# A hybrid encoder layer on one core: both S5 runs one behind the other in the projection phase, beside the delta rule of block 0

## The chip, the core and the metric

The kernel runs on one core of one Trainium2 chip. The core has five engines with a queue each: TensorE (PE, its weight loads PEld), VectorE (DVE), ScalarE (ACT), GpSimd (POOL) and SyncE (SP), whose queue issues the DMAs here. Instructions of one queue start in order; between queues there are semaphores. The metric is the device time of one execution in microseconds, lower is better.

## What is computed

One layer of a streaming encoder for 2048 prompt tokens and 32 sample tokens, in float32, width 1024. All head groups read the same normalised input through one projection:

```python
hn = rmsnorm(h, norm_mix)
qkv_pre, z, ba, u5, cc = split(hn @ w_in)
ya = gdn_mixer(qkv_pre, z, ba, ...)    # A: gated delta rule, 4 heads x 128, state carried along the tokens
yb = s5_mixer(u5, ...)                 # B: 16 x 64 complex states, scan along the tokens, GELU, GLU
yc = conformer_conv(cc, ...)           # C: GLU, causal depthwise convolution of width 31, LayerNorm, swish
h = h + concat([ya, yb, yc]) @ w_out
hf = rmsnorm(h, norm_ffn)
h = h + (silu(hf @ w1) * (hf @ w3)) @ w2        # 22 x 128 hidden columns
h = h + (p @ pe_w) * sigmoid(h @ pe_gate)
y = rmsnorm(h, norm_final)
```

Outputs are y for both token groups and the last states of the three mixers.

## The kernel before

**Blocks and phases.** The prompt is cut into four blocks of 512 tokens (NB = 4); the 32 sample tokens ride with block 3, whose rows are 544 wide. A first phase (PhaseA) projects block after block with w_in; a second (PhaseF) does output projection, FFN and gated embedding, block after block. Between them stand the heads: the conformer (`conformer_block`), the delta rule (`gdn_group`, two groups of 256 tokens per block, one more for the sample tokens behind block 3) and S5 (`s5_unit`, one run for two blocks, G.UB = 2, so G.NU = 2 runs). The delta rule and S5 carry a state, so their blocks come in order. Everything passes between phases through DRAM: `G.us` to S5, `G.xcd` to the conformer, `G.sild` to the delta rule, `G.mixT[b]` from the heads to the output projection of block b.

**Matmuls.** Each projection (`dense`, L122) is three passes of float32r matmuls with 512 columns: high weight half by high input half, low by high, high by low. The high half of a weight is made on ScalarE (L94). The low half is subtracted (L98) by GpSimd, for w3 by VectorE, when a weight is first used, that is in block 0; it is then kept in DRAM and loaded in later blocks. A projection's result lies in one of three PSUM banks (`psD`) until VectorE or ScalarE has read it.

**What sets the order.** Heads are Python generators (chains). `dense` counts the columns that it issues; each time these reach `G.stage` (7168, and 9216 in block 0 of PhaseF), every chain goes one step on, and `yield k` makes a chain wait k steps. `G.flush` runs chains on without columns between until its condition holds. Instructions recorded so are then set in each engine's queue by a scheduler that goes by priorities and by its own estimate of when operands are there; so a head's instructions can stand some way from where they were recorded.

**Chains before.** In PhaseA one chain sets up S5's constants, opens the S5 memory (`R("s5_0")`, a pool named w5 here), and in it runs conformer and delta rule of block 0. From block 2 on a second chain runs S5 for blocks 0 and 1 in that memory. `G.flush()` finishes both. In PhaseF one chain goes on: conformer 1, delta rule 1, conformer 2, S5 for blocks 2 and 3 (in a memory of its own), delta rule 2, conformer 3, delta rule 3 with the sample tokens. Block b of PhaseF starts after `ready[0] >= b`.

**Lines that the prediction speaks of.** L826 (L827 after the change) is the conformer's convolution: 62 VectorE instructions per block, each on half of the 256 channels, written `cacc<-xc,cc_w,cacc`; its input `xc` is loaded at L813. They stand in VectorE's queue among the additions that empty PSUM: L1173 (`hb<-hb,ps_d`, output projection), L1196 to L1204 (hidden columns), L1218 (down projection), L1242 and L1243 (gate). L78 makes the low halves `fal` of the FFN's inputs, L1167 the sum of squares, and L134 spreads the resulting scale. L1069 to L1109 (`ps_vn` to `ps_ot`) are the end of the delta rule. S5's matmuls are L468 (`ps_v`), L526 and L527 (`ps_y`) and L556 (`ps_glu`). L668 is the first matmul of a block in PhaseA; its inputs `hh` and `hl` are made by L77 and L78 into the pool `xp`.

Of the kernel before, what the change touches and what calls it, by code (L numbers as in the profile page):

```python
# [423 lines left out]
def s5_unit(G, A, u, wp, pspool):  # L424
# [14 lines left out]
    for jq in range(4):  # L439
# [15 lines left out]
        Gm = ld("G", [P, 2, 2, P], G.s5c["G"][:, js])  # L455
        Toep = ld("Toep", [P, 4, P], G.s5c["Toep"][:, jq * 4:jq * 4 + 4])

        yield 3

        w = [wp.tile([P, 2, NCT], F32, tag=f"w{i}", name=f"w{i}") for i in range(2)]  # L460
        tm = [wp.tile([P, 2, NCT], F32, tag=f"tm{i}", name=f"tm{i}") for i in range(4)]
# [50 lines left out]
                else:  # L512
                    V.tensor_copy(S1[half[h], js, i], X[h][half[i], :, NC])

        yield 4

        ys = wp.tile([P, 4, NCT], F32, tag="ys", name="ys")
        ysv = ys.rearrange("p (j h) c -> p j h c", h=2)
# [17 lines left out]
        jh = jq // 2  # L536
# [7 lines left out]
        nc.scalar.activation(t, t, AF.Tanh, scale=math.sqrt(2.0 / math.pi))  # L544
        nc.scalar.activation(yf, yf, AF.Copy, scale=0.25)
        V.scalar_tensor_tensor(gq[:, jh], t, 1.0, yf, op0=ALU.add, op1=ALU.mult)
        yield 1 if jh == 0 else 5
    spc = 512 // NCT
    for j in range(2):
        yb = wp.tile([P, n], F32, tag="yf", name="yb")  # L550
# [12 lines left out]
        for i in range(G.UB):  # L563
            b = u * G.UB + i
# [7 lines left out]
class PhaseA:  # L572


    def __init__(self, G, A, ctx):
        self.G, self.A = G, A
        nc = G.nc
        V = nc.vector
        E = lambda name, bufs=1, **k: ctx.enter_context(G.tc.tile_pool(name=name, bufs=bufs, side="left", reuse_waits="tile", **k))
        self.wp = E("aw", 2)  # L580
        self.xp = E("ax", 12)
        cp = E("ac")

        def const(nm, shp, src):
            t = cp.tile(shp, F32, tag=nm, name=nm)
            nc.sync.dma_start(t, src)
            return t

        self.gm = const("gmix", [P, KD], A.norm_mix)
        self.cw = G.cw  # L590
        wr = G.wraw.tile([P, KD, 8], F32, tag="wr", name="wr_ba")
        nc.sync.dma_start(wr, A.w_ba)
        self.wba = cp.tile([P, KD, 16], F32R, tag="wba", name="wba")
        nc.scalar.activation(self.wba[:, :, 0:8], wr, AF.Copy)
        nc.gpsimd.tensor_tensor(self.wba[:, :, 8:16], wr, self.wba[:, :, 0:8].bitcast(F32), op=ALU.subtract)
        self.tails = cp.tile([P, 12, 3], F32, tag="tails", name="tails")
        nc.gpsimd.memset(self.tails, 0.0)
        self.taild = const("taild", [P, 12, 3], A.st_gconv)
# [34 lines left out]
    def block(self, b):  # L633
        G, A, wp = self.G, self.A, self.wp
# [71 lines left out]
        for j, ur in enumerate(urs):  # L706
            u = wp.tile([P, L5, n // L5], F32, tag="gacc", name="u5")
            V.tensor_tensor(u, ur.rearrange("p (c s) -> p s c", s=L5), bc.rearrange("p (c s) -> p s c", s=L5), op=ALU.mult)
            co = (b % G.UB) * BLK // L5
            nc.sync.dma_start(G.us[b // G.UB][:, j * P:(j + 1) * P, co:co + n // L5].rearrange("s p c -> p s c"), u)  # L710

        for j in range(2):
            wg = load_weight(G, A.w_in[20 + j], KD, "ccg", j)
# [544 lines left out]
def trunk_kernel(ctx: ExitStack, tc: tile.TileContext, A):  # L1258
    nc = tc.nc
    G = Ctx()  # L1260
# [16 lines left out]
            tc.cur_priority = G.pr[old]  # L1277

    G.chains = []
    G.acc = 0  # L1280

    def advance(c):
# [28 lines left out]
    NB = G.NB  # L1311
    E = lambda name, bufs=1, **k: ctx.enter_context(tc.tile_pool(name=name, bufs=bufs, **k))
# [59 lines left out]
    R = lambda name, bufs=1: tc.tile_pool(name=name, bufs=bufs, side="right", reuse_waits="tile")  # L1372

    def conf(b, wp):
        return conformer_block(G, A, b, wp, G.psM)

    def gdn_part(b, i, S, sp):
        S = yield from gdn_group(G, A, sp, G.psM, G.tp_, b * 4 + 2 * i, P, 2, S, b, 256 * i)
        if b == NB - 1 and i == 1:
            nc.sync.dma_start(A.gdn_p, S)  # L1380
            Sd = G.kp.tile([P, NH, P], F32, tag="S", name="Sd0")
            nc.sync.dma_start(Sd, A.st_gdn)
            Sd = yield from gdn_group(G, A, sp, G.psM, G.td_, 0, TS, 1, Sd, b, BLK)
            nc.sync.dma_start(A.gdn_s, Sd)
        return S
# [3 lines left out]
    def conf_of(b):  # L1389
        with R(f"cc_{b}") as wp:  # L1390
            yield from conf(b, wp)

    def s5_of(u):
        with R(f"s5_{u}") as wp:
            yield from s5_unit(G, A, u, wp, G.psM)

    def gdn_of(b):
        with R(f"gd_{b}", 2) as sp:
            for i in range(2):
                state[0] = yield from gdn_part(b, i, state[0], sp)  # L1400

    def run(*gens):

        for g in gens:
            yield from g

    with ExitStack() as cx:
        pa = PhaseA(G, A, cx)
        pa.block(0)

        box = {}

        def first_s5():
            while "w5" not in box:
                yield 1
            yield from s5_unit(G, A, 0, box["w5"], G.psM)
            box["done"] = True

        def first_heads():
            with R("s5i") as tp:  # L1420
                yield from s5_init(G, A, tp, G.psM)
            with R("s5_0") as w5:
                box["w5"] = w5
                yield from conf_of(0)
                yield from gdn_of(0)
                while "done" not in box:
                    yield 1

        G.start(first_heads())
        for b in range(1, NB):  # L1430
            if b == G.UB:
                G.start(first_s5())
            pa.block(b)
        if NB == G.UB:
            G.start(first_s5())
        G.flush()
    pf = PhaseF(G, A, ctx)
    ready = [0]

    def later_heads():  # L1440
        for b in range(1, NB):
            yield from conf_of(b)
            if b % G.UB == 0:
                yield from s5_of(b // G.UB)
            yield from gdn_of(b)
            ready[0] = b

    G.start(later_heads())
    for b in range(NB):
        G.flush(lambda: ready[0] >= b)  # L1450
        G.stage = STAGE.get(b, STAGE["A"])
        pf.block(b)

# [114 lines left out]
```

## Time and profile before

| | |
|---|---|
| median of 3 runs | 2884.57 us (2880.83 to 2887.48) |
| profiled execution | 2888.11 us, its span 2886.3 us, mean granted clock 0.979 |
| TensorE busy | 2763.9 us (96%) |
| VectorE busy | 1751.6 us (61%) |
| ScalarE, GpSimd busy | 935.2 us (32%), 549.4 us (19%) |
| DMA queue of SyncE | 562.7 MB, 60.4% of 16 engines' span |
| TensorE on the chain that ended last | 64%, of it the projections L122 57% |

PhaseA ends at about 682 us, and the blocks of PhaseF at about 1231, 1779, 2320 and 2886 us. The page gives busy time per engine, then the span in 40 slices (each digit tenths of a slice), then groups of instructions by line, engine and tiles (`out<-in`, x the count). A busy TensorE is not TensorE at its peak, since a matmul's shown time overlaps the next one's; so stretches are best read by how many matmuls they hold and how long they last. A row of a wait gives the engine and the line that waited, what released it, total us, times, and the longest.

### The profile page before, as it was taken

How to read it: one execution, taken by the hardware profiler on the slowest of the kernel's cores; microseconds unless marked ns; L12 is line 12 of the kernel's file. 1: busy time of each engine (PE TensorE's matmuls, PEld its weight loads, DVE VectorE, ACT ScalarE, POOL GpSimd, SP SyncE). 2: the span in 40 equal slices, each digit the busy share in tenths (PEclk: the TensorE clock that was granted, in tenths of full speed). 3: DMA queues.
4: the chain of work that ended last, by engine and by line, in shares of the span. 5: the costliest groups of instructions: out<-in, count | busy, mean ns of one | idle time of the engine just before them, and what ended most of it. 6: DMA issues, size and time to landing. Idle time of an engine off the chain costs nothing.

```text
span 2886.3 us, 41015 instructions
## 1 busy us (share of the span) xinstructions
PE 2763.9 (96%) x15300; PEld 2359.9 (82%) x15300; DVE 1751.6 (61%) x3933; ACT 935.2 (32%) x1409; POOL 549.4 (19%) x460
## 2 busy tenths in 40 slices
PE   7899999999999999899999999999999979999997
PEld 5668778898878887688888887778888869999997
DVE  8969765865675847966563755856464733333343
ACT  4243423313422222343422333342332423222232
POOL 5731312234232323421010101000010110000000
PEclk9999999999999999999999999999999979999998
DMA  6578777657654555487665657566565654555553
GB/s 225 170 252 269 248 227 227 199 181 245 206 185 167 190 168 200 152 288 220 216 183 176 187 174 242 187 207 192 172 193 154 197 193 149 174 175 176 175 187 107
DMA packets 278919, 565.32 MB, mean 196 GB/s; under 512 B 67344, under 2 KB 126880, under 8 KB 278576
## 3 DMA queue, kind: packets, MB, share of 16 engines
q1 hardware_dynamic: 278720, 562.70, 60.4%
q8 instruction: 121, 1.98, 0.3%
q14 instruction: 78, 0.64, 0.1%
HBM read 457.76 MB, written 104.25 MB: 195 GB/s over the span
## 4 chain that ended last, share of the span: by engine, by line
PE 64%; DVE 8%; DMA 3%; issue 3%; SPq 1%; ACT 1%; POOL 0%; DVEq 0%; POOLq 0%; ACTq 0%
PE ps_d L122 57%; DVE cacc L826 3%; PE ps_kk L935 1%; PE ps_q L1013 1%; PE ps_z L1026 1%; DVE ct L982 1%; DVE cx L983 1%; DVE hb L1218 1%; DMA xd<-cx 1%; DMA hb<-mixT 1%; PE ps_vn L1069 0%; PE ps_o L1083 0%; PE ps_o L1084 0%; PE ps_s L1076 0%; PE ps_ks L1056 0%
## 5 line engine op out<-in xcount | busy, mean ns | idle before, releaser
L94 ACT ACTIVATE wh_w<-wr_w 128x1024 fp32r<-128x1024 f32 (+1 forms) x272 | 281.3, 1034 | 762.9 <-PE ps_d L122 551.4
L122 PE MATMUL ps_d<-fah,wh_w 128*128 128x512 f32 (+1 forms) x1760 | 379.4, 354 | 7.4 <-DVE fa L1196 2.9
L122 PE MATMUL ps_d<-fal,wh_w 128*128 128x512 f32 (+1 forms) x1760 | 376.5, 353 | 0.0
L122 PE MATMUL ps_d<-fah,wl_w 128*128 128x512 f32 (+1 forms) x1760 | 376.1, 353 | 0.0
L122 PEld LDWEIGHTS ps_d<-fah,wh_w 128*128 128x128 f32 x1760 | 291.1, 189 | 53.6 <-issue 4.0
L122 PEld LDWEIGHTS ps_d<-fal,wh_w 128*128 128x128 f32 x1760 | 291.4, 189 | 43.2
L122 PEld LDWEIGHTS ps_d<-fah,wl_w 128*128 128x128 f32 x1760 | 291.3, 189 | 43.2 <-issue 0.4
L1218 DVE TENSOR_TENSOR hb<-hb,ps_d 128x512 f32<-128x512 f32 (+1 forms) x240 | 139.7, 583 | 167.1 <-PE ps_d L122 166.7
L122 PE MATMUL ps_d<-acth,wh_w 128*128 128x512 f32 (+1 forms) x880 | 210.3, 355 | 9.1 <-DVE hb L1218 7.7
L122 PE MATMUL ps_d<-acth,wl_w 128*128 128x512 f32 (+1 forms) x880 | 210.1, 354 | 0.0
L122 PE MATMUL ps_d<-actl,wh_w 128*128 128x512 f32 (+1 forms) x880 | 208.6, 354 | 0.0
L826 DVE SCALAR_TENSOR_TENSOR cacc<-xc,cc_w,cacc 128x512 f32<-128x512 f32 (+1 forms) x240 | 189.4, 824 | 0.0
L122 PEld LDWEIGHTS ps_d<-acth,wh_w 128*128 128x128 f32 x880 | 148.6, 189 | 34.7 <-DVE hb L1218 6.1
L122 PEld LDWEIGHTS ps_d<-actl,wh_w 128*128 128x128 f32 x880 | 149.4, 189 | 22.2
L122 PEld LDWEIGHTS ps_d<-acth,wl_w 128*128 128x128 f32 x880 | 149.2, 189 | 22.2
L98 POOL TENSOR_TENSOR wl_w<-wr_w,wh_w 128x1024 fp32r<-128x1024 f32 (+1 forms) x46 | 108.2, 2351 | 253.9 <-ACT wh_w L94 226.3
L1201 DVE SCALAR_TENSOR_TENSOR fth<-ps_d,bc 128x512 f32<-128x512 f32 (+1 forms) x110 | 64.8, 589 | 132.0 <-PE ps_d L122 131.3
L1196 DVE TENSOR_TENSOR fa<-ps_d,bc 128x512 f32<-128x512 f32 (+1 forms) x110 | 64.5, 588 | 118.5 <-PE ps_d L122 109.4
L122 PE MATMUL ps_d<-hh,wh_qkv 128*128 128x512 f32 (+1 forms) x480 | 107.2, 365 | 13.8 <-DVE raw L615 13.0
L1204 DVE TENSOR_TENSOR actl<-fa,acth 128x512 fp32r<-128x512 f32 (+1 forms) x110 | 81.3, 739 | 51.3 <-ACT acth L1203 50.9
L1199 DVE SCALAR_TENSOR_TENSOR fa<-fth,fa 128x512 f32<-128x512 f32 (+1 forms) x110 | 73.1, 667 | 58.8 <-ACT fth L1198 58.6
L122 PE MATMUL ps_d<-hh,wl_qkv 128*128 128x512 f32 (+1 forms) x480 | 105.5, 361 | 2.3 <-POOL wl_qkv L98 2.3
(479 smaller groups left out, 4783.3 us busy)
## 6 DMA issues: line engine op xcount, KB each, us to landing
wr_w<-in_w SPq DMA_DIRECT2D x256, 512.0 KB, 4.3
wl_w<-lo_w SPq DMA_DIRECT2D x192, 512.0 KB, 4.0
lo_w<-wl_w SPq DMA_DIRECT2D x64, 512.0 KB, 2.9
wr_qkv<-in_w_in SPq DMA_DIRECT2D x48, 512.0 KB, 4.7
wl_qkv<-lo_qkv SPq DMA_DIRECT2D x36, 512.0 KB, 4.2
wr_out<-in_w_out SPq DMA_DIRECT2D x32, 512.0 KB, 5.2
wr_gate<-in_pe_gate SPq DMA_DIRECT2D x32, 512.0 KB, 4.3
wl_out<-lo_out SPq DMA_DIRECT2D x24, 512.0 KB, 5.9
```

The costliest lines, as they stand in the source:

```text
L94: nc.scalar.activation(wh, wr, AF.Copy)
L98: e.tensor_tensor(wl, wr, wh.bitcast(F32), op=ALU.subtract)
L122: nc.tensor.matmul(ps[:, :cn], a[:, i, :], x(k)[:, c0:c0 + cn], start=start and p_ == 0 and i == 0, stop=stop and p_ == 2 and i == K - 1)
L826: V.scalar_tensor_tensor(acc[:, j], xc[:, j, t:t + W], cn_.w[:, j, t:t + 1], acc[:, j], op0=ALU.mult, op1=ALU.add)
L935: nc.tensor.matmul(kk4[:, h - h0], kq[:, 2 * h, cw], kq[:, 2 * h:2 * h + 2, cw], start=True, stop=True)
L982: V.tensor_tensor(t, cx[:, 0:nq, j:j + 1].to_broadcast(sh), cu[:, j:j + 1, j + 1:].to_broadcast(sh), op=ALU.mult)
L983: V.tensor_tensor(cx[:, 0:nq, j + 1:], cx[:, 0:nq, j + 1:], t, op=ALU.subtract)
L1196: V.tensor_tensor(a, p1[:, :cn], bc[:, cs], op=ALU.mult)
L1199: V.scalar_tensor_tensor(a, th, 1.0, a, op0=ALU.add, op1=ALU.mult)
L1201: V.scalar_tensor_tensor(th, p3[:, :cn], 0.5, bc[:, cs], op0=ALU.mult, op1=ALU.mult)
L1204: V.tensor_tensor(fb[:, cs], a, fa[:, cs].bitcast(F32), op=ALU.subtract)
L1218: V.tensor_tensor(hb[m][:, c0:c0 + cn], hb[m][:, c0:c0 + cn], p_[:, :cn], op=ALU.add)
```

## The change

Both S5 runs are made by one chain (`s5_chain`) in one memory, w5. It starts before block 2 of PhaseA; a run starts when the blocks that it needs have been projected, for which PhaseA counts them (`G.u5`). The heads chain (`heads_chain`) runs conformer and delta rule of block 0 beside it, holds w5 until both runs are through, and only then goes on with conformer 1, delta rule 1 and so on; S5 no longer stands between conformer 2 and delta rule 2. The second phase starts when block 0's heads and the first run are ready. Three of the waits inside a run are one step shorter. The pool of PhaseA's input halves has 11 buffers for each half where it had 12.

```diff
@@ s5_unit
-        yield 3
+        yield 2
...
-        yield 4
+        yield 3
...
-        yield 1 if jh == 0 else 5
+        yield 1 if jh == 0 else 4
@@ PhaseA
-        self.xp = E("ax", 12)
+        self.xp = E("ax", 11)
...
+        G.u5 = b + 1
@@ trunk_kernel
+    box = {"ready": -1, "runs": 0}
+
+    def s5_chain():
+        while "w5" not in box:
+            yield 1
+        for u in range(G.NU):
+            while G.u5 < (u + 1) * G.UB:
+                yield 1
+            yield from s5_unit(G, A, u, box["w5"], G.psM)
+            box["runs"] = u + 1
+
+    def ready(b):
+        return box["ready"] >= b and box["runs"] * G.UB > b
+
+    def heads_chain():
+        with R("s5i") as tp:
+            yield from s5_init(G, A, tp, G.psM)
+        with R("s5_0") as w5:
+            box["w5"] = w5
+            yield from conf_of(0)
+            yield from gdn_of(0)
+            box["ready"] = 0
+            while box["runs"] < G.NU:
+                yield 1
+        for b in range(1, NB):
+            yield from conf_of(b)
+            yield from gdn_of(b)
+            box["ready"] = b
...
-        G.start(first_heads())
+        G.start(heads_chain())
         for b in range(1, NB):
-            if b == G.UB:
-                G.start(first_s5())
+            if b == min(G.UB, NB - 1):
+                G.start(s5_chain())
             pa.block(b)
...
-        G.flush()
+        G.flush(lambda: ready(0))
...
-            yield from conf_of(b)
-            if b % G.UB == 0:
-                yield from s5_of(b // G.UB)
-            yield from gdn_of(b)
-            ready[0] = b
...
-        G.flush(lambda: ready[0] >= b)
+        G.flush(lambda: ready(b))
```

Line numbers behind `PhaseA.block`'s new line are one higher than before, up to the chains.

The first place is VectorE's queue in block 0 of PhaseF, from the last output projection to the scale for the hidden columns: `hb` is the addition, `fal` the low halves, `ssum` the sum of squares, `rms_v` to `rso` the scale. Before:

```order
L1173 TENSOR_TENSOR hb<-hb,ps_d 128x512
L98 TENSOR_TENSOR wl_w_7324<-wr_w_7321,wh_w_7323 128x1024
L1167 TENSOR_TENSOR ssum_6921<-ssum_6921,sq_7222 128x512
L78 SCALAR_TENSOR_TENSOR fal<-hb,g_6861,fah 128x512 x5
L1173 TENSOR_TENSOR hb<-hb,ps_d 128x512
L78 SCALAR_TENSOR_TENSOR fal<-hb,g_6861,fah 128x512 x2
L1167 TENSOR_TENSOR ssum_6921<-ssum_6921,sq_7263 128x512
L78 SCALAR_TENSOR_TENSOR fal<-hb,g_6861,fah 128x512
L864 SCALAR_TENSOR_TENSOR cxn<-cth,cxn 128x512
L154 TENSOR_SCALAR rms_v<-ps_ss 128x4
```

And in the changed kernel, from the last of these additions on:

```order
L1174 TENSOR_TENSOR hb<-hb,ps_d 128x512
L78 SCALAR_TENSOR_TENSOR fal<-hb,g_7389,fah 128x512 x2
L827 SCALAR_TENSOR_TENSOR cacc<-xc,cc_w,cacc 128x512
L78 SCALAR_TENSOR_TENSOR fal<-hb,g_7389,fah 128x512
L827 SCALAR_TENSOR_TENSOR cacc<-xc,cc_w,cacc 128x512
L1168 TENSOR_TENSOR ssum_7449<-ssum_7449,sq_7793 128x512
L78 SCALAR_TENSOR_TENSOR fal<-hb,g_7389,fah 128x512
L827 SCALAR_TENSOR_TENSOR cacc<-xc,cc_w,cacc 128x512 x8
L154 TENSOR_SCALAR rms_v<-ps_ss 128x4
L827 SCALAR_TENSOR_TENSOR cacc<-xc,cc_w,cacc 128x512 x2
```

The convolution of conformer 1 has moved here; before, it stood among the projections of block 3 in PhaseA. All 62 of its instructions stand between the third output projection of block 0 and the second hidden column.

The second place is TensorE's queue at the end of block 2, with the sample tokens' delta rule (`ps_vn` to `ps_ot`) and the first matmuls of block 3 (`wh_out`, 272 columns). Before:

```order
L122 MATMUL ps_d<-fal,wh_gate 128x512 x8
L1069 MATMUL ps_vn<-rk,X 32x128 x4
L151 MATMUL ps_ss<-ones,ssum_20261 128x1 x4
L1076 MATMUL ps_s<-vn,rk 128x128 x4
...
L134 MATMUL ps_bc<-ident,rso 128x128 x4
L1109 MATMUL ps_ot<-ident,o 128x32 x4
L122 MATMUL ps_d<-fah,wh_out 128x272 x22
```

And in the changed kernel, first where `ps_ot` stands now, then the end of the block:

```order
L122 MATMUL ps_d<-fah,wh_gate 128x512 x7
L1110 MATMUL ps_ot<-ident,o 128x32 x4
L122 MATMUL ps_d<-peh,wh_pe 128x512 x2
...
L122 MATMUL ps_d<-fal,wh_gate 128x512 x8
L122 MATMUL ps_d<-fah,wh_out 128x272 x8
L122 MATMUL ps_d<-fah,wl_out 128x272 x8
```

The end of the delta rule has moved from behind the block's last gate column to its first one, and block 3's output projection follows block 2's last gate column directly.

The third place is TensorE's queue at the first matmuls of the second S5 run. Before, in block 1 of PhaseF:

```order
L122 MATMUL ps_d<-fah,wl_out 128x512 x8
L122 MATMUL ps_d<-fal,wh_out 128x512
L468 MATMUL ps_v<-ug,c_PT 64x132 x8
L122 MATMUL ps_d<-fal,wh_out 128x512 x7
L122 MATMUL ps_d<-fah,wh_out 128x512 x8
```

And in the changed kernel, in block 3 of PhaseA:

```order
L122 MATMUL ps_d<-hl,wh_cca 128x272 x8
L122 MATMUL ps_d<-hh,wh_ccg 128x272 x3
L468 MATMUL ps_v<-ug,c_PT 64x132 x8
L122 MATMUL ps_d<-hh,wh_ccg 128x272 x5
L122 MATMUL ps_d<-hh,wl_ccg 128x272 x8
```

The run has moved from the output projection of block 1 into the conformer's columns of block 3; its last matmuls (`ps_glu`) now stand among the last columns of PhaseA.

More of the change, by code (lines that the diff above doesn't have):

```diff
@@ L1279, in trunk_kernel @@
     G.chains = []
+    G.u5 = 0
     G.acc = 0
@@ L1391, in conf_of @@
             yield from conf(b, wp)
-    def s5_of(u):
-        with R(f"s5_{u}") as wp:
-            yield from s5_unit(G, A, u, wp, G.psM)
     def gdn_of(b):
@@ L1409, in trunk_kernel @@
         pa.block(0)
[L1411 to L1427, printed above, removed]
-        G.start(first_heads())
+        G.start(heads_chain())
         for b in range(1, NB):
-            if b == G.UB:
-                G.start(first_s5())
+            if b == min(G.UB, NB - 1):
+                G.start(s5_chain())
             pa.block(b)
-        if NB == G.UB:
-            G.start(first_s5())
-        G.flush()
+        if NB == 1:
+            G.start(s5_chain())
+        G.flush(lambda: ready(0))
     pf = PhaseF(G, A, ctx)
-    ready = [0]
-    def later_heads():
-        for b in range(1, NB):
-            yield from conf_of(b)
-            if b % G.UB == 0:
-                yield from s5_of(b // G.UB)
-            yield from gdn_of(b)
-            ready[0] = b
-    G.start(later_heads())
     for b in range(NB):
-        G.flush(lambda: ready[0] >= b)
+        G.flush(lambda: ready(b))
         G.stage = STAGE.get(b, STAGE["A"])
```

## The prediction

> **What bounds the kernel now.** I read the page first: the span, the engines' shares, and the slices.
>
> ```profile
> span 2886.3 us, 41015 instructions
> PE 2763.9 (96%) x15300; PEld 2359.9 (82%) x15300; DVE 1751.6 (61%) x3933; ACT 935.2 (32%) x1409; POOL 549.4 (19%) x460
> PE   7899999999999999899999999999999979999997
> PEclk9999999999999999999999999999999979999998
> ```
>
> TensorE is the bound nearly everywhere, and the change removes none of its work. What it can win or lose are the places where TensorE waits: the start, a slice in the middle, and the slice near 2300 us, where the granted clock falls too. To see what a stretch loses I need the price of the work in it. The chain of waits has long unbroken runs of the projection matmul, and the timeline has the small ones:
>
> ```profile
> 688.00 41.50 PE ps_d L122 x180
> 2235.96 1.05 PE L1056 MATMUL ps_ks<-S,kq 128*128 128x128 f32 x8
> ```
>
> That is 41.50 / 180 = 0.2306 us for one projection matmul of 512 columns, and 0.13 us for a small one. Now three stretches, with all instructions (first three rows: length, PE with its count, PEld, DVE, ACT, POOL, clock) and with the projections alone (last three):
>
> ```profile
> 682.00:755.00 73.00, 71.28 (x319) 56.75 (x318) 45.53 (x60) 32.87 (x50) 31.31 (x19) 1.00 0.73 253
> 1108.00:1231.00 123.00, 107.83 (x445) 83.49 (x444) 106.32 (x129) 41.17 (x62) 52.50 (x28) 0.96 0.55 191
> 1779.00:1860.00 81.00, 74.25 (x315) 59.04 (x316) 76.69 (x112) 29.95 (x43) 11.22 (x8) 0.96 0.70 243
> ...
> 682.00:755.00 73.00, 69.18 (x291) 53.71 (x291) 8.05 (x13) 0.00 (x0) 1.00 0.73 253
> 1108.00:1231.00 123.00, 106.95 (x429) 81.69 (x428) 17.58 (x26) 4.12 (x7) 0.96 0.55 191
> 1779.00:1860.00 81.00, 71.89 (x291) 56.31 (x292) 7.97 (x12) 0.58 (x1) 0.96 0.70 243
> ```
>
> The first is the output projection and the first hidden columns of block 0: 291 x 0.2306 = 67.1, 28 small ones 3.6, so 2.3 us of 73 are lost. The third is the same piece of block 2: 67.1 and 3.1, so 10.8 of 81 are lost. The second is the end of block 0: 98.9 and 2.1, so 22 of 123 are lost. What sets them apart is the conformer's depthwise convolution, 62 VectorE instructions on one accumulator, which lies in the second stretch (head 2) and the third (head 3). VectorE works nearly without pause there (106 of 123, 77 of 81), and TensorE waits for the additions that stand behind the convolution in VectorE's queue.
>
> The slice near 2300 us is the end of block 2. The waits of TensorE between 2255 and 2397 us, a window of that place, and the ordinary wait at the same step of block 1 to 2 (last row):
>
> ```profile
> PE ps_ot L1109 <- DVE o L1101: 10.1, 1, 10.1
> PE ps_d L122 <- ACT fah L1134: 5.9, 2, 5.7
> PE ps_vn L1069 <- DMA X<-xd: 4.4, 1, 4.4
> ...
> 2320.50:2354.60 34.10, 18.09 (x71) 12.77 (x70) 15.80 (x29) 6.95 (x11) 10.63 (x8) 0.50 0.53 185
> ...
> PE ps_d L122 <- ACT fah L1134: 3.9, 2, 3.2
> ```
>
> The last delta rule, that of the 32 sample tokens, ends after the last matmul of block 2, and block 3 cannot start without it: 10.1 + 4.4 + 5.7 = 20.2 us of waiting, and 34.1 us in which TensorE is granted half its clock.
>
> **The change, part by part.** The sum is made against the profiled execution's own time, 2888.1 us, which lies 3.5 us above the median of 2884.57; the difference that I find is then taken off the median. The three runs shown lie 6.7 us apart, so a measurement tells about 0.2% (5.8 us) from no change.
>
> *The heads chain of the last phase gets shorter: -25.* Without the second S5 run the chain is shorter, and in the order the last transpose of the sample tokens now stands 227 projection matmuls, 227 x 0.2306 = 52 us, before the end of block 2. The three waits (20.2) go, but for the 3.9 that block 1 to 2 shows as ordinary; the 18.1 us of TensorE work at half clock would take 9.0. So 20.2 - 3.9 + 9.0 = 25. Next late there is the splitting of block 3's inputs, which is the 3.9 kept. Ends: -20 and -28. The Trainium skill ("TensorE: Matmul & The Clock Gate", What's actually happening) says that the clock is halved after about 3.4 us without work and given back after as long a busy stretch; the row agrees on the half, and by that rule a kept wait of over 3.4 us would leave part of the 9.0 standing.
>
> *The convolution of head 1 moves: +17.* Before, it ran in block 3 of the projection phase; now it waits for the S5 memory and lies in block 0's output projection. What it costs by place, in min/median/max of one multiply-add in ns (head 1 in the projection phase, head 2 at the end of block 0, head 3 at the start of block 2), and their sums for 60:
>
> ```profile
> L826 DVE SCALAR_TENSOR_TENSOR cacc<-xc,cc_w,cacc x60: 710/732/746, 564.4 to 616.7; 128x512 f32<-128x512 f32 x60
> L826 DVE SCALAR_TENSOR_TENSOR cacc<-xc,cc_w,cacc x60: 733/739/2892, 1128.5 to 1206.3; 128x512 f32<-128x512 f32 x60
> L826 DVE SCALAR_TENSOR_TENSOR cacc<-xc,cc_w,cacc x60: 798/803/812, 1790.6 to 1859.5; 128x574 f32<-128x574 f32 x60
> ...
> 564.00:617.00 53.00, 41.62 (x60) 0.97 0.68 215
> 1127.00:1207.00 80.00, 58.74 (x60) 0.94 0.47 162
> ```
>
> In block 0, and only there, GpSimd makes the low halves of the weights, and single multiply-adds take up to 2892 ns. The same is seen on the sums of squares of the very stretch to which head 1 moves, beside the other work of VectorE and GpSimd there:
>
> ```profile
> 708.88 2.40 POOL L98 TENSOR_TENSOR wl_out<-wr_out,wh_out 128x1024 fp32r<-128x1024 f32 x1 [3.06 <-ACT wh_out L94]
> ...
> 703.61 2.76 DVE L1167 TENSOR_TENSOR ssum<-ssum,sq 128x512 f32<-128x512 f32 x1 [0.97 <-ACT sq L1166]
> 724.02 0.69 DVE L1173 TENSOR_TENSOR hb<-hb,ps_d 128x512 f32<-128x512 f32 x1 [1.39 <-PE ps_d L122]
> 725.16 1.22 DVE L98 TENSOR_TENSOR wl_w<-wr_w,wh_w 128x1024 fp32r<-128x1024 f32 x1 [0.45 <-ACT wh_w L94]
> 726.30 0.68 DVE L1167 TENSOR_TENSOR ssum<-ssum,sq 128x512 f32<-128x512 f32 x1
> 728.01 3.40 DVE L78 SCALAR_TENSOR_TENSOR fal<-hb,g,fah 128x512 fp32r<-128x512 f32 x5 [1.03 <-PE ps_d L122]
> 739.51 0.16 DVE L154 TENSOR_SCALAR rms_v<-ps_ss 128x4 f32<-128x4 f32 x1 [2.49 <-PE ps_ss L151]
> ```
>
> By the new order VectorE has, from the third addition of the output projection to the first hidden column: 49 multiply-adds x 0.74 = 36.3, 5 additions x 0.69 = 3.5, 6 sums of squares x 0.68 = 4.1, 8 low halves x 0.68 = 5.4, 3 weight halves x 1.22 = 3.7, 4 small ones 0.6: 53.5 us. TensorE has 192 matmuls and 8 small ones there, 45.3 us, and then stops for the scale that ends this chain. So it waits at least 8 us; five GpSimd subtractions lie inside, and each holds VectorE by up to 2.76 - 0.68 = 2.1, 10 us more. The loading of the convolution's input, for which VectorE's whole queue waits, can add up to 5, as the chain of waits shows it for head 1:
>
> ```profile
> 558.06 5.08 DMA xc<-xcd
> ```
> Less the 2.3 lost there already: between +6 and +21. I take +17, nearer the upper end, since the row of head 2 under the same GpSimd work shows 58.74 - 60 x 0.739 = 14.4 us of such holding. In the place that it leaves, block 3's VectorE time is taken by the second S5 run.
>
> The Trainium skill ("SBUF — State Buffer", Who interferes with whom) states that a VectorE instruction with two SBUF inputs and a GpSimd instruction that reads SBUF exclude each other for the whole instruction. The 2.76 beside 2.40 agrees, and the rule speaks against this move; by it alone the term would lie at the upper end.
>
> *Heads 2 and 3: -6 and +3, and 0.* Head 3's convolution leaves block 2's start: 81 against 73 us, so at most -8; the delta rule that now lies there takes some back, -6. It goes to the end of block 1, without GpSimd's subtractions: 0 to +7, I take +3. Head 2's convolution stays at the end of block 0, but starts some 30 instructions later, among the gate columns. Those have, for each column of 30 matmuls (6.9 us), 7 multiply-adds and three others, 7.2 us: as much too long per column as before in fewer columns. I take 0 against the 22 lost now, ends -6 and +6.
>
> *The second S5 run itself: +5.* Its instructions are the same. What TensorE waited for in the first run, in the projection phase (first two rows), and in the second, in block 1 (last):
>
> ```profile
> PE ps_v L468 <- DMA c_PT<-s5PTre: 2.4, 1, 2.4
> PE ps_v L468 <- DMA c_PT<-s5PTim: 1.8, 1, 1.8
> ...
> PE ps_y L527 <- DVE X L507: 0.3, 1, 0.3
> ```
>
> So a run costs 4 us of waiting there and almost none in block 1. Its last step, the GLU, now stands among the last matmuls of the phase, about 46 of them (10.6 us) behind the load that starts its chain. Ends 0 and +13, the upper one if each of its four quarters and the GLU wait as the worst above (2.4). DMAs that SyncE issues for it stand before weight loads; in block 1 they stood so too.
>
> *One buffer less for the block's inputs: +1.* At the steps to the next block TensorE waits little for them:
>
> ```profile
> PE ps_d L668 <- ACT hh L77: 1.3, 2, 0.8
> ```
>
> One more split behind the last buffer's release may double that; 0 to +2. *Earlier mixer outputs: -2.* Block 1's delta rule ends some 490 matmuls earlier before block 2, so part of the 3.9 goes; 0 to -3. The flags and the new conditions issue nothing on the chip.
>
> Sum: -25 + 17 - 6 + 3 + 0 + 5 + 1 - 2 = -7. The profiled execution would take 2881, the median 2878 us.
>
> **The rivals.** *VectorE's new collision decides (slower).* Place: block 0's output projection. The 49 multiply-adds are held at each subtraction, the input comes 7 us late, and the 13 multiply-adds left over (9.6 us) delay the first hidden columns as well: 8 + 10 + 7 + 10 = 35 instead of 17, so +11, 2896. It turns the sign from a term of +30 on, that is when the stretch of 73 us becomes longer than 103. For it: VectorE is already busy for 77 of 81 us in block 2's like stretch, without GpSimd. Against: there only 10.8 were lost.
>
> *The collision is hidden (faster by more).* TensorE can go on by the banks that it has free, and only +6 stays; head 2 gains 6: -7 - 11 - 6 = -24, 2861. For it: 2.3 us lost in block 0 now although VectorE is held there too.
>
> *The projection phase gives the gain back (no change).* The second run costs +13, as the DMA share is higher there: +1, 2886. For it: the waits on S5's constants. Against: VectorE's work in the phase stays about equal, one convolution against one run.
>
> **How the numbers follow.** The forecast has 0.50, and its own spread of about 9 us falls to 0.30 below the bound of 5.8 and 0.20 within it; the hidden collision 0.17, the phase's loss 0.11, the deciding collision 0.22. So faster 0.47, same 0.31, slower 0.22. The range reaches into both far rivals, 2855 to 2899, with about one in ten left out on each side.
>
> **What would show it.** Right: no 10 us wait for the last transpose and no half clock of 34 us before block 3; block 0's first 291 projections take about 90 us; head 1's multiply-adds show maxima above 2 us. Wrong: that stretch under 80 or over 103 us; waits of the second S5 run above 10 us; or the gap before block 3 staying because the sample tokens' chain is late again.

## The result, and the profile after it

The change made the kernel slower by about half a per cent: 2901.23 us median of 4 runs (2900.05 to 2902.98) against 2885.98 us (2880.83 to 2887.48) for the kernel before. The ratio is 1.0057, its 95% interval 1.0039 to 1.0074. The forecast was 2878, and 2901 lies just outside its range.

The page of the changed kernel, the same rows as of before:

```profile
span 2900.6 us, 40975 instructions
PE 2767.2 (95%) x15300; PEld 2357.3 (81%) x15300; DVE 1748.0 (60%) x3933; ACT 934.6 (32%) x1409; POOL 537.9 (19%) x460
PE   7799989998899999989999999999999999999997
PEclk9899999999999999999999999999999999999998
```

The slice near 2300 us that fell to 7 is filled, and the clock with it. But a slice near 400 us and two between 653 and 798 us have fallen from 9 to 8. The matmuls are the same 15300; so the question is only where TensorE waits. The timeline gives the start of each block's first output matmul, and with the span's end it makes a table of stages (us; the last two kernels are experiments below):

| stage | before | after | 12 buffers | 12 buffers, old pauses |
|---|---|---|---|---|
| projection phase, to the first output matmul | 682.7 | 731.7 | 710.4 | 709.0 |
| block 0 | 548.0 | 560.9 | 561.0 | 546.3 |
| block 1 | 548.6 | 539.7 | 539.0 | 533.0 |
| block 2, with the gap behind it | 568.0 | 532.1 | 530.7 | 533.8 |
| block 3 | 539.0 | 536.2 | 536.0 | 538.3 |
| span | 2886.3 | 2900.6 | 2877.1 | 2860.4 |

The second S5 run leaves block 1 and comes to the projection phase, so part of the first row's growth of 49.0 is its own work. What that is, the groups of its matmuls in block 1 of the kernel before show (count, busy time, mean ns of one):

```profile
L526 PE MATMUL ps_y<-ug,c_Toep 128*128 128x128 f32 (+1 forms) x64 | 11.2, 253 | 0.0
L556 PE MATMUL ps_glu<-gq,glu 128*128 128x396 f32 (+1 forms) x24 | 8.2, 459 | 0.0
L527 PE MATMUL ps_y<-X,c_G 128*128 128x128 f32 x32 | 6.6, 288 | 0.3 <-DVE X L507 0.3
L527 PE MATMUL ps_y<-XD,c_G 128*128 128x4 f32 x32 | 5.8, 253 | 0.0
L468 PE MATMUL ps_v<-ug,c_PT 128*64 128x132 f32 x64 | 4.7, 284 | 0.0
```

These busy times overlap (36.5 us together); from each start to the next they make about 23 us. So the phase should have grown by 23 and the 6 us of waiting that I forecast for the run and the missing buffer, 29 in all. It grew by 49: some 20 us are not in my sum.

The end of block 2 is as forecast. TensorE's waits from 2290 to 2420 us in the changed kernel:

```profile
PE ps_d L122 <- ACT gth L1242: 0.7, 1, 0.7
PE ps_ss L151 <- DVE ssum L1168: 0.4, 1, 0.4
PE ps_d L122 <- ACT fah L1135: 0.2, 1, 0.2
```

No wait for the last transpose is left. Block 0's output projection is as forecast too. The stretch of before was 73 us for 291 projections; here it is in the changed kernel, all instructions first, then the projection matmuls alone, below them head 1's multiply-adds (min/median/max ns), TensorE's two longest waits there, and VectorE's wait for the convolution's input:

```profile
731.60:822.60 91.00, 75.16 (x306) 59.76 (x305) 82.41 (x103) 28.11 (x40) 31.24 (x13) 0.91 0.50 177
...
731.60:822.60 91.00, 73.37 (x292) 0.91 0.50 177
...
L827 DVE SCALAR_TENSOR_TENSOR cacc<-xc,cc_w,cacc x60: 730/738/2899, 756.6 to 828.7; 128x512 f32<-128x512 f32 x60
...
PE ps_d L122 <- ACT fah L77: 7.0, 1, 7.0
PE ps_bc L134 <- DVE rso L70: 5.1, 1, 5.1
...
755.05 1.00 DVE L825 TENSOR_SCALAR cacc<-xc,cc_w,cc_b 128x512 f32<-128x512 f32 x2 [4.98 <-DMA xc<-xcd]
```

The same number of projections takes 91 us, 18 more than before, where I took 17 more. VectorE is busy for 82.4 of them (45.5 of 73 before), single multiply-adds take up to 2899 ns, and the clock is 0.91. TensorE's two waits, 12.1 us, are for the hidden columns' inputs, which ScalarE makes from what VectorE's additions leave, and for their scale, the end of VectorE's chain. (Two expectations below say 99 us for this stretch: that was a window with 320 projections.)

That left the projection phase. TensorE's longest waits in it, 188 to 730 us, in the changed kernel:

```profile
PE ps_v L468 <- DMA ug<-us: 7.6, 2, 5.1
PE ps_v L468 <- DMA c_PT<-s5PTre: 7.2, 1, 7.2
PE ps_d L668 <- ACT hh L77: 4.5, 4, 3.6
PE ps_d L122 <- DVE zz L744: 3.4, 3, 1.3
```

From this view I took the first two rows for the cause: 14.8 us for the loads of the S5 runs (9.7 of them in the second run), where the kernel before had 4.2. The change had shortened three pauses of the run, one of them right behind these loads, and I had not priced that at all. That was **theory A**. Its rivals: **B**, SyncE's queue is too full in this phase, whatever the pauses; **C**, the missing input buffer, which I had priced at 1 us. For the output projection the question was **D**, whether GpSimd's subtractions or VectorE's own sum made the 18 us.

### The profile page after: what moved, and what is told of

It is laid out like the page before. It is cut to its first block, busy times and chain, and to the rows that moved or that the text cites. A ratio compares the mean times of both kernels' runs of the same rounds, so it can differ in the third digit from the quotient of the medians.

```text
span 2900.6 us, 40975 instructions
## 1 busy us (share of the span) xinstructions
PE 2767.2 (95%) x15300; PEld 2357.3 (81%) x15300; DVE 1748.0 (60%) x3933; ACT 934.6 (32%) x1409; POOL 537.9 (19%) x460
## 4 chain that ended last, share of the span: by engine, by line
PE 70%; DVE 16%; DMA 8%; issue 2%; ACT 2%; SPq 1%; POOL 1%; DVEq 0%; ACTq 0%; POOLq 0%
PE ps_d L122 61%; DVE cacc L827 4%; DMA xk<-in_xT 1%; DVE cx L984 1%; DMA xc<-xcd 1%; DVE gacc L625 1%; PE ps_q L1014 1%; PE ps_kk L936 1%; DVE ct L983 1%; PE ps_z L1027 1%; DMA mixT<-zy 1%; DMA cu<-ud 1%; DVE fal L1137 1%; PE ps_o L1084 1%; PE ps_o L1085 1%
## 5 line engine op out<-in xcount | busy, mean ns | idle before, releaser
L827 DVE SCALAR_TENSOR_TENSOR cacc<-xc,cc_w,cacc 128x512 f32<-128x512 f32 (+1 forms) x240 | 200.3, 870 | 0.0
L122 PEld LDWEIGHTS ps_d<-acth,wh_w 128*128 128x128 f32 x880 | 148.4, 188 | 27.7 <-issue 5.3
L1204 ACT ACTIVATE acth<-fa 128x512 fp32r<-128x512 f32 (+1 forms) x110 | 60.3, 548 | 141.1 <-DVE fa L1203 141.0
```

The source lines that it names most:

```text
L122: nc.tensor.matmul(ps[:, :cn], a[:, i, :], x(k)[:, c0:c0 + cn], start=start and p_ == 0 and i == 0, stop=stop and p_ == 2 and i == K - 1)
L827: V.scalar_tensor_tensor(acc[:, j], xc[:, j, t:t + W], cn_.w[:, j, t:t + 1], acc[:, j], op0=ALU.mult, op1=ALU.add)
L1204: nc.scalar.activation(fa[:, cs], a, AF.Copy)
```

## The experiments

All medians in us; the ratio is to the kernel before in the same job, with its 95% interval.

| kernel | median | ratio | interval |
|---|---|---|---|
| changed kernel | 2901.23 | 1.0057 | 1.0039 to 1.0074 |
| before, 11 buffers | 2903.01 | 1.0067 | 1.0055 to 1.0079 |
| before, 10 buffers | 2901.5 | 1.0053 | 1.0035 to 1.0070 |
| before, short pauses | 2897.03 | 1.0042 | 1.0030 to 1.0054 |
| before, one t2 buffer less | 2884.94 | 1.0001 | 0.9990 to 1.0012 |
| changed, block 3's delta rule held back | 2930.56 | 1.0153 | 1.0139 to 1.0167 |
| changed, no GpSimd in the output projection | 2888.87 | 1.0009 | 1.0000 to 1.0017 |
| changed, 12 buffers | 2881.53 | 0.9988 | 0.9980 to 0.9997 |
| changed, old pauses | 2876.64 | 0.9970 | 0.9958 to 0.9981 |
| changed, 12 buffers, convolution held back | 2867.01 | 0.9935 | 0.9914 to 0.9956 |
| changed, 12 buffers, old pauses | 2864.46 | 0.9927 | 0.9914 to 0.9940 |
| the last one, S5 loads from ScalarE's queue | 2869.85 | 0.9951 | 0.9932 to 0.9971 |

**The missing buffer alone.** The kernel before with one number changed:

```diff
-        self.xp = E("ax", 12)
+        self.xp = E("ax", 11)
```

> The kernel before with 11 instead of 12 buffers for the projection phase's inputs, and nothing else. My term for it was +1 (0 to +2): 2886 to 2888. Theory C (the missing buffer makes each block's first matmuls late, as the 3.6 us wait for hh at the start of the fourth block of the changed kernel suggests): +5 to +10, 2891 to 2896.

Measured: 2903.01, 19 us more, above what even theory C gave. The whole loss of the changed kernel is no larger. In its trace the first output matmul comes at 697.3 instead of 682.7, and all stages behind it are as before; so 14.6 of the 14.9 us between the two profiled spans are lost in the projection phase. How, the start of the fourth block shows. A block needs eight splits of its inputs (`hh` on ScalarE, `hl` on VectorE); with twelve buffers four of them find room early, with eleven three. The last split of the kernel before, and then, at the same step with 11 buffers, a row of ScalarE and the last split behind it:

```profile
511.20 0.73 ACT L77 ACTIVATE hh<-xk,gmix 128x544 fp32r<-128x544 f32 x1
```

```profile
522.99 1.06 ACT L541 ACTIVATE gu<-yf 128x1024 f32<-128x1024 f32 x1 [3.38 <-DMA yf<-yd]
524.95 0.74 ACT L77 ACTIVATE hh<-xk,gmix 128x544 fp32r<-128x544 f32 x1
```

The split comes 13.8 us later; only 4.0 of these are the block's own later start (its first matmul at 509.8 instead of 505.8). Its input is loaded later, and in ScalarE's order it stands behind S5's GELU, for whose data the queue waits 3.4 us. The load itself, in SyncE's queue, before and then with 11 buffers:

```profile
506.62 0.37 SPq L646 DMA_DIRECT2D xk<-in_xT  x1
```

```profile
518.50 0.55 SPq L646 DMA_DIRECT2D xk<-in_xT  x1
```

VectorE's queue stands still for the splits (3.10 and 2.80 us), its delta-rule work waits behind them, and TensorE, in order too, waits for that (first column the start, second the length with its gaps, the last what ended the wait):

```profile
516.94 0.79 DVE L78 SCALAR_TENSOR_TENSOR hl<-xk,gmix,hh 128x544 fp32r<-128x544 f32 x1 [3.10 <-ACT hh L77]
525.72 1.40 DVE L78 SCALAR_TENSOR_TENSOR hl<-xk,gmix,hh 128x544 fp32r<-128x544 f32 x1 [2.80 <-ACT hh L77]
...
516.96 0.56 PE L668 MATMUL ps_d<-hh,wba 128*16 128x272 f32 x2 [2.54 <-ACT hh L77]
523.07 4.12 PE L935 MATMUL ps_kk<-kq 128*128 128x256 f32 x8 [3.78 <-DVE AQ L945]
```

In 25 us of this place TensorE is busy for 18.67 at a mean clock of 0.80; 25 us of the same place before had 23.72 at full clock:

```profile
505.00:530.00 25.00, 18.67 (x89) 13.38 (x88) 16.95 (x38) 10.63 (x16) 11.46 (x8) 0.80 0.57 173
```

```profile
500.00:525.00 25.00, 23.72 (x159) 19.96 (x158) 17.49 (x35) 11.88 (x20) 10.61 (x8) 1.00 0.63 196
```

**A second buffer less.** The same line with 10.

> The kernel before with 10 input buffers, two less than it had. With 11 it took 19 us more. If every split of the next block's inputs that falls behind the block's end costs (each late split holds up VectorE's and ScalarE's queues at three block starts), a second one costs as much again: 2915 to 2925. If the 19 us came from one unlucky place in the order at 11, the second costs little: 2895 to 2908.

Measured: 2901.5, no more than with 11. So the cost is not so much per late split. It is a step between 12 and 11. That it hangs on whether a split falls behind other chains' work in the queues, and not on how many do, is my reading; which of the rearranged rows is worth how many of the 19 us stays open.

**The short pauses alone.** The kernel before with the three pauses of the change:

```diff
-        yield 3
+        yield 2
...
-        yield 4
+        yield 3
...
-        yield 1 if jh == 0 else 5
+        yield 1 if jh == 0 else 4
```

> The kernel before with the three shortened pauses alone (2, 3 and 4 steps). The second S5 run stays in block 1 and the gap before block 3 stays. Theory A (the pauses are the cause): TensorE's waits for ug and c_PT in the projection phase rise from 4.2 us to 10 or more with the first run alone, and the kernel takes 2892 to 2900. Theory B (the place of the second run is the cause): the waits stay within 3 us of before, and the time within 5 us of 2886.

Measured: 2897.03, 12 to 13 us more, as theory A had it, but not by its mechanism. The loss lies in the projection phase: the first output matmul comes at 695.1 us instead of 682.7. TensorE's waits from 190 to 730 us:

```profile
PE ps_cf L856 <- POOL ctk L853: 8.5, 1, 8.5
...
PE ps_v L468 <- DMA sild<-raw: 2.3, 1, 2.3
```

The waits of `ps_v` for its loads are no longer than before (3.2 against 4.2 us). What is new is a hole at the end of the phase. First the last transposes of block 0's delta rule in the kernel before; then the same with the short pauses, and what TensorE does from 680.7 us to the first output matmul:

```profile
667.63 0.60 PE L1109 MATMUL ps_ot<-ident,o 128*128 128x128 f32 x4
```

```profile
678.45 0.60 PE L1109 MATMUL ps_ot<-ident,o 128*128 128x128 f32 x4
...
689.19 2.30 PE L856 MATMUL ps_cf<-ident,ctk 128*128 128x128 f32 x8 [8.45 <-POOL ctk L853]
695.08 5.49 PE L122 MATMUL ps_d<-fah,wh_out 128*128 128x512 f32 x12 [3.59 <-ACT fah L1134]
```

The delta rule ends 11 us later, right at the last projection of the phase, and block 0's output projection has to wait until its result has been written and loaded. The 8.5 us are part of that hole: the last matmuls of conformer 1 (`ps_cf`) stand there, and wait for a chain behind the end of the delta rule in VectorE's queue. The pauses cost by moving other work, not by their lead. Why the delta rule ends later was not tried.

**The old pauses in the changed kernel.** The same three lines the other way round.

> The changed kernel with the three pauses of the S5 run as they were before (3, 4 and 5 steps instead of 2, 3 and 4). In the new order the second run then goes on into block 0's output projection, head 1's convolution lies behind it, and the last transposes of the sample tokens stand some 24 matmuls before the end of block 2 instead of some 200. Theory A (the shortened pauses leave the S5 loads too little lead: TensorE waits 14.8 us for ug and c_PT in the projection phase against 4.2 before): these waits fall to 5 us or less and the phase ends some 20 us sooner. Theory B (two S5 runs fill SyncE's queue in this phase whatever the pauses): the waits stay at 12 us or more. By both, the first 291 projections of block 0 shorten from 99 us to 80 to 90, and 15 to 25 us of the waiting before block 3 come back. Sum from 2901: A 2885 to 2895, B 2903 to 2915.

Measured: 2876.64, 25 us less than the changed kernel, and 8 to 9 under the lower end of A. The S5 waits fell to 5.2 us, as A said, and the phase ended 12 us sooner, not 20. Most came elsewhere: the second run ends later, so head 1's convolution starts behind the output projection (at 807 instead of 755 us), and block 0 takes 547.2 instead of 560.9 us. And one expectation failed: the gap before block 3 did not come back. There, in the waits from 2270 to 2385 us, the longest is the ordinary one:

```profile
PE ps_d L122 <- ACT fah L1135: 4.3, 1, 4.3
```

24 matmuls (24 x 0.2306 = 5.5 us) between the last transposes and the end of the block are enough to leave no more than that.

**The gap put back.** A pause in the changed kernel's heads chain:

```diff
             yield from conf_of(b)
+            if b == 3:
+                yield 90
             yield from gdn_of(b)
```

> The changed kernel with a pause of 90 steps ahead of the delta rule of block 3, so that the last transposes of the sample tokens stand again right at the end of block 2; nothing before block 1's last hidden columns moves. If the gap before block 3 was worth what I took for it, the 10 us wait for the transpose and the stretch of half clock come back and the kernel takes 20 to 28 us more than the changed one: 2921 to 2929. Rival (the gain at this place came from elsewhere, as from head 3's convolution): under +8.

Measured: 2930.56, 29 us more than the changed kernel. The waits before block 3 and the stretch behind them are those of the kernel before, to within 0.5 us:

```profile
PE ps_ot L1110 <- DVE o L1102: 10.1, 1, 10.1
PE ps_d L122 <- ACT fah L1135: 6.1, 2, 5.7
PE ps_vn L1070 <- DMA X<-xd: 4.9, 1, 4.9
...
2362.60:2396.70 34.10, 17.80 (x71) 12.69 (x70) 15.30 (x29) 6.94 (x11) 10.62 (x8) 0.50 0.52 183
```

So the gap is worth 29 us. I had 25, because I kept 3.9 us of waiting for the split of block 3's inputs; the changed kernel shows 0.2 there, and 20.2 + 9.0 makes 29.2.

**No GpSimd in the output projection.** ScalarE writes zeros for these low halves; the products lack them.

```diff
-            e = nc.vector if name == "w3" else nc.gpsimd
-            e.tensor_tensor(wl, wr, wh.bitcast(F32), op=ALU.subtract)
+            if name == "out" or (name == "w1" and key < 4):
+                nc.scalar.activation(wl, wr, AF.Copy, scale=0.0)
+            else:
+                e = nc.vector if name == "w3" else nc.gpsimd
+                e.tensor_tensor(wl, wr, wh.bitcast(F32), op=ALU.subtract)
```

> The changed kernel in which GpSimd makes no low halves of block 0's output weights and first four w1 columns: ScalarE writes zeros there instead, so those products lack their low halves; the order on VectorE and TensorE stays. Theory D (GpSimd's subtractions hold VectorE: a convolution step takes 881 ns there on average against 740): the steps go back to some 740 ns, the first 291 projections of block 0 shorten from 99 us to 80 to 86, and the kernel takes 2883 to 2891. Rival (VectorE's own sum of 53 us against TensorE's 45 is what costs): at most 4 us, 2897 or more.

Measured: 2888.87, 12 us less. The multiply-adds, in their new stretch, no longer vary:

```profile
L830 DVE SCALAR_TENSOR_TENSOR cacc<-xc,cc_w,cacc x60: 740/744/753, 747.9 to 808.7; 128x512 f32<-128x512 f32 x60
...
723.80:803.00 79.20, 71.40 (x291) 0.96 0.55 199
```

The maximum falls from 2899 to 753 ns, and the 291 projections (last row) from 91 to 79.2 us. (D's 80 to 86 was meant for the window with 320 projections; that takes 85.9 us here, at the upper end.) So of the 18 us about 12 come from GpSimd. They come through VectorE: none of TensorE's waits in the stretch was for a low half that GpSimd makes. The other 6 are what VectorE's own sum and its 5 us wait for the convolution's input leave; no run takes these two apart. The kernel's 12 us are not the stretch alone: in the profiled execution the projection phase also ends 7.8 us sooner, and block 1 is 2.6 us longer. The rule of the Trainium skill ("SBUF — State Buffer", Who interferes with whom), that such a VectorE instruction and a GpSimd one that reads SBUF exclude each other, agrees with the two rows of the multiply-adds.

**Twelve buffers in the changed kernel.** The room comes from the delta rule's tiles `Ds` and `vn`, which share the tag `t2` and get one buffer instead of two:

```diff
-        self.xp = E("ax", 11)
+        self.xp = E("ax", 12)
...
-        Ds = sp.tile([P, NH, nt], F32, tag="t2", name="Ds")[:nt]
+        Ds = sp.tile([P, NH, nt], F32, tag="t2", name="Ds", bufs=1)[:nt]
...
-        vn = sp.tile([P, NH, P], F32, tag="t2", name="vn")[:nt]
+        vn = sp.tile([P, NH, P], F32, tag="t2", name="vn", bufs=1)[:nt]
```

> The changed kernel with its 12 input buffers back; the room for them comes from one delta-rule buffer (t2) that is there once instead of twice. Theory C (the missing buffer is what I mis-sized): it alone costs 15 to 19 us in the projection phase, so the changed kernel falls from 2901 to 2880 to 2887, and the waits for hh at the start of the second and the fourth block go back to what they were before. Theory A (the pauses alone): no more than 5 us, 2896 or more.

> The control for the two kernels with 12 input buffers: the kernel before with the one t2 buffer less alone. The order hardly differs, so 2884 to 2889; if the delta rule needs that buffer, it is more, and has to be taken off the other two.

Measured: 2881.53, 20 us less than the changed kernel, and 2884.94 for the control, no change. The phase falls from 731.7 to 710.4, 27.7 longer than before, where the S5 run's own 23 and my 6 make 29. By the first matmul of the fourth block (508.8 us instead of 521.8) 13 of these 21 us are there already, so in this kernel the buffer costs at more than one place. TensorE's waits for `hh` fall from 4.5 to 2.6 us (1.6 before), and the S5 waits from 14.8 to 7.8 us without a change of the pauses: a good part of them followed from the missing buffer.

**Both undone.** Twelve buffers and the old pauses.

> The changed kernel with both undone: 12 input buffers (one t2 buffer less) and the old pauses 3, 4, 5. If the two costs are separate, their gains add: 2877 less 15 to 19 is 2858 to 2862, faster than before by 0.8 to 0.9 per cent. If they are one and the same (either one alone disturbs the order of the phase), 2873 to 2880.

Measured: 2864.46, 2 us above the range for separate costs. The two gains add for the most part: alone they were 25 and 20 us, together they are 37, so with the old pauses the buffer brings 12 us and not 20. This is the fastest kernel of the study, 0.73% under the one before (0.6 to 0.86%): the change's move of the S5 run, without what was given up for it (one `t2` buffer is, which costs nothing).

**The convolution held back instead.** Twelve buffers and the short pauses; head 1's convolution, and with it the chain of heads behind it, may start only behind the scale of block 0's output projection:

```diff
+    if b == 1:
+        nc.gpsimd.tensor_copy(xc[:, 0, 0:1], G.gate[0][:, 0:1])
...
         rc, _ = rms_bcast(G, wp, G.psN, "pn", ssum, n, None)
+        G.gate[b] = rc
...
+            while b == 1 and 0 not in G.gate:
+                yield 1
             yield from conf_of(b)
```

> The changed kernel with 12 input buffers (one t2 buffer less), its short pauses, and one thing more: GpSimd writes one column of head 1's convolution input from the scale that ends block 0's output projection, so that this convolution can only start behind it. The S5 runs stay as in the changed kernel. Theory E (the pauses cost by the place that they give to the convolutions, not by the lead of the S5 loads): nearly the whole step from 2881.5 to 2864.5 that the old pauses brought comes by this alone, 2860 to 2870. Theory A (the lead of the S5 loads): only the rest of the collision in the output projection goes, and later places move as with the old pauses; at most 8 us, 2873 or more.

Measured: 2867.01; the interval of its ratio holds that of the old pauses (0.9935, 0.9927). Theory E stands: with 12 buffers, about 15 of the pauses' 17 us are the place of the convolutions. In the table of stages the old pauses gain in block 0 (561.0 to 546.3) and block 1 (539.0 to 533.0), while the projection phase moves by 1.4 only; here the same two stages take 548.5 and 533.9. In both kernels not only head 1's convolution has moved: head 2's begins at 1264 and 1269 us, in block 1, and no longer at the end of block 0 (1214 us, where block 1 begins at 1271).

**The S5 loads on another queue.** `nc.sync.dma_start` becomes `nc.scalar.dma_start` for `ug`, `PT` and the other constants, in the kernel with both undone.

> The fastest kernel so far (12 input buffers, old pauses) with the loads of the S5 runs, ug, PT and the other constants, issued from ScalarE's queue instead of SyncE's. Theory B (in the projection phase the S5 loads stand too far back in SyncE's queue): TensorE's 8.8 us of waits for ug and PT fall to 3 or less and with the half clock behind them 8 to 12 us go: 2852 to 2857. Rival (the transfers themselves are slow, at a DMA share of 0.7 to 1.0, or the buffers come free too late): no more than 3 us, 2861 to 2868; should ScalarE's queue stand still for these loads, slower.

Measured: 2869.85, no gain (the intervals of the two ratios overlap). Theory B's first half came true and its second did not. The waits from 188 to 709 us:

```profile
PE ps_q L1014 <- DVE XT L993: 11.2, 2, 6.4
PE ps_gc L794 <- DVE tp_ekd L801: 3.4, 1, 3.4
...
PE ps_v L468 <- DMA c_PT<-s5PTim: 0.9, 1, 0.9
```

The wait for the S5 loads is down from 8.8 to 0.9 us, and the delta rule's transposed matrix (`XT`) is waited for in its place, 11.2 us. Why it comes later there wasn't tried.

## Why the prediction was wrong

By its own steps:

- **The gap before block 3, -25.** Right, a little small: its return costs 29. The 3.9 us that I kept were not there.
- **Head 1's convolution, +17.** Right for the stretch, which grew by 18: 12 through GpSimd, where I had 10, and 6 for VectorE's own sum and the wait for its input, where I had 8 and up to 5, all ahead of subtracting the 2.3 lost already. One reading behind it paired the wrong rows: beside the sum of squares of 2.76 us at 703.61 stand three GpSimd subtractions in one row (698.22, 7.60 us), and the row shown, at 708.88, stands beside a sum of 2.47 us at 709.36. The size of the holding is hardly touched by that.
- **Heads 2 and 3, and the earlier mixer outputs, -6 + 3 + 0 - 2.** Block 0 as a whole grew by only 12.9, so behind the stretch it got some 5 us shorter, where I had put head 2 at 0. Block 1 got 8.9 us shorter, where the +3 and the S5 run's 23 make 20, and block 2 got 35.9 shorter, where -25 - 6 - 2 make 33. Block 3, for which I had no term, is 2.8 shorter. No run takes these apart; that they nearly cancel is luck.
- **The second S5 run's own waits, +5 (0 to +13).** Near it with 12 buffers, 6.8 us. In the changed kernel they are 12.3: 9.7 for its loads, the rest for its own chain. As the pauses are the same in both, the difference follows from the next point.
- **One buffer less, +1 (0 to +2).** This is the step that failed. "At the steps to the next block TensorE waits little for them": I read the 1.3 us that TensorE waits for `hh` with twelve buffers (the longest wait 0.8) as if they bounded what eleven would cost. It is the row of a wait that the buffers keep short, not of one that they cause. It measured 19 us in the kernel before and 20 in the changed one. That is nearly the whole difference of 23 us between the forecast and the result: with 12 buffers the changed kernel takes 2881.53 against 2885.42, 4 less, where I had forecast 7. (The profiled spans differ by 9.2; but the profiled execution with 12 buffers is the fastest of eleven, and that of before took longer than any of its four other runs.)
- **The pauses.** The prediction didn't price them. They cost 12 to 13 us in the kernel before, by a late end of block 0's delta rule, and 17 (with 11 buffers 25) in the changed one. There most of it lies inside the convolution's +17: the shorter run is what lets the convolution start in the output projection. So the collision that I priced as part of the move was a choice that the move didn't need.
- **The rivals.** The time is that of an outcome on the slower side, but not of its mechanism: the stretch in question took 91 us, not over 103. The rival that came nearest is the third, the projection phase that gives the gain back, by 20 us and not by 8, and through the buffer. The first rival's sign would turn at a term of +24, a stretch of 97 us: the sum without the convolution is -24. The +30 and 103 that I gave are where the slower time could be told from no change.
- **The signs.** All three signs of being right came true: no wait for the last transpose, 91 us, maxima of 2899 ns. Of the signs of being wrong one came true, the second S5 run's waits above 10 us. None of them looked at the buffer, the term that failed.

Shown by experiment are the cost of the gap and of the buffer, the share of GpSimd and the place of the convolutions. Argued from one trace alone is how the late split runs through the three queues; where the buffer costs in the changed kernel stays open.

## What to carry to other kernels

A buffer that is given up to make room is to be priced by the work that it lets run ahead, not by the wait that is left when it is there: look which instruction would come late, and what stands behind it in each in-order queue. A change that makes room for its main part with small cuts elsewhere deserves one run for each cut alone; here the two cuts (together 37 us) hid a gain of about 20. And where a chain of work is moved, look at what starts behind its end: the pauses mattered for where other work fell, the convolutions in the changed kernel and the end of the delta rule in the one before.

## What the runs showed of the hardware

In this kernel the cost of input buffers was a step: 12 to 11 cost 19 us, 11 to 10 nothing (2903.01, 2901.5). Zeros written by ScalarE beside VectorE's multiply-adds did not disturb these (753 ns at most), GpSimd's subtractions did (2899 ns). And 5.5 us between the last transposes and the end of a block were enough to hide all but 4.3 us of waiting of a chain whose lateness cost 29 us.
